# Other ranks in the instruction planner of a four-layer decoder trunk, two lead tiles in the second MLP and an earlier sigmoid table

## The chip, the cores and the metric

The kernel runs on one core of a Trainium2 chip. The metric is device time in microseconds (us) of one execution, the median of several runs; one further execution is profiled. TensorE (PE in the profile) does the matmuls and has a separate row for its weight loads (PEld), VectorE is DVE, ScalarE is ACT, GpSimd is POOL, and SyncE (SP) only issues the loads and stores (DMAs). Each engine works through its own queue in order and waits at an instruction until what that instruction needs is there.

## What is computed

The reference is a trunk of four layers over 512 positions, with 16 learned positions put in front (528 in all), at width 1024, in float32. Cut to what matters:

```python
def sq_relu_mlp(h, norm_g, w_up, w_down):
    return jnp.square(jax.nn.relu(rms_norm(h, norm_g) @ w_up)) @ w_down

def conformer_conv_module(...):
    u = rms_norm(h, norm_g) @ pw1_w + pw1_b
    u = u[..., :CONF_DIM] * jax.nn.sigmoid(u[..., CONF_DIM:])
    u = causal_depthwise_conv(u, dw_w, dw_b)
    u = jax.nn.silu(layer_norm(u, ln_g, ln_b))
    return u @ pw2_w + pw2_b

def reference(...):
    h = jnp.concatenate([meta, x], axis=1)
    for layer in range(DEPTH):                 # DEPTH = 2
        if layer % 2 == 0:
            h = h + even_mixer(...)            # one input projection, sliding-window attention
        else:                                  # beside an SSD scan, one output projection
            h = h + conformer_conv_module(...)
        h = h + sq_relu_mlp(...)               # 1024 -> 4096 -> 1024
    return h[:, N_META:]
```

The weights of the two MLPs are most of the work: 4096 x 1024 up and down for each.

## The kernel before, in words

**Tiles and streams.** The positions lie in the free dimension and the features on the partitions. They are split in two streams, A (s = 0, blocks 0 to 2, 272 positions) and B (s = 1, blocks 3 and 4, 256 positions); the second MLP works on 256 of each. The trace names tiles by stage, layer, quarter and stream: up02A is the up projection of layer 0, quarter 2, stream A, dn02A the down projection behind it, pw the two projections of the conformer module, out those of the output projection.

**Precision.** A linear layer is computed in split form: a weight tile of 128 x 1024 (or 128 x 512) is loaded by SP (`wr`, L289), ACT casts it to its high part (`wh`, L280, in `th_cast`), and DVE (L254) or POOL (L256) subtracts to get the low part (`wl`, in `th_low`). An output tile of 128 features is 24 matmuls at L308 for eight k of 128: per k the high part times the high and the low part of the input (nh and nl, or ah and al), then the low weight part times the high input. A stage of eight tiles is 192 matmuls.

**The planner.** No engine's order is written by hand. `Sched` holds threads (Python generators) which offer their next operation. `step` takes the operation that can start first by the planner's costs, among equals the one with the smaller rank (the second argument of `spawn`), then the one that waited longest; what it takes is appended to that engine's queue. An operation with a `late` of LATE (600 ns) is put off by that margin, so that PE does not stand waiting for its input. The matrix stages are the thread `main` (rank 5), the weight loads have rank 0, the casts 1, and the low parts 0 or 4, according to how many split pieces stand ready; each finished tile spawns an evacuation with a rank of its own.

**Banks.** Outputs stand in PSUM. `pmm` gives a stage one of three mm banks or, in the later stages, one of the three bg banks besides: four at most. A bank comes free with the last instruction of the evacuation that reads it. In `mlp` the evacuation of an up tile is DVE (relu, L268, or L261 with the row norm), ACT (square), ACT (cast to ah) and DVE (al, L254). In `prep`, for stages that add to the residual stream, it goes on to nh, nl, h and the sum of squares, DVE's acc being last.

**dense.** `dense` (L462 to L512) runs a stage. With `lead` tiles it starts so many tiles on their first `cut` k's, each in its own bank, and then finishes them one after the other, so that PE has work before the last k's of the input are written. The other tiles follow one at a time. In the second MLP the lead was 4 and the cut 6.

**Norms.** A stage that writes the residual stream also gathers sums of squares. `row_norm` (L530) sums them over the partitions by a matmul into a bank (names st and a key), takes the reciprocal root by ACT's Sqrt and a Newton step on DVE (`rsqrt`), and spreads the result over the partitions by a second matmul whose copy is `rb`. Keys: in0 and in1 for the first layer's input, nx for the first MLP, cn for the conformer module, ln for its layer norm, fn for the second MLP. Sigmoid and Sqrt stand in different tables of ACT, and a change of table shows as ACT_TABLE_LOAD.

**Stages.** `main` runs: the input projection; out for stream A; quarters 0 and 1 of the first MLP for A, beside which the attention (att_a, att_b, att_c) and the SSD scan (ssd_...) of blocks 3 and 4 still run; then, when these are done, the memory pool that they used is closed, a pool for whole weight tiles is opened in its place (`wp`), and out for B begins (L1312 its evacuation); quarters 2 and 3 for A; pw1 for A; the first MLP for B; pw1 for B; pw2 for A; the second MLP for A; pw2 for B; the second MLP for B, which writes the output.

Of the kernel before, what the change touches and what calls it, by code (L numbers as in the profile page):

```python
# [53 lines left out]
LATE = 600.0  # L54
# [11 lines left out]
class Sched:  # L66
# [106 lines left out]
    def spawn(self, gen, prio, name):  # L173

        self.threads.append([gen, prio, None, None, 0, name])
# [55 lines left out]
def trunk(ctx: ExitStack, tc: tile.TileContext, h0, vecs, cmat, atab, atab0, w_in, w_dt, w_out,  # L231
# [86 lines left out]
    def BM(*ms):  # L318
        return MM(ms, LATE)
# [148 lines left out]
    def dense(name, nts, tot, xs, evac, lead=0, cut=0, when=None):  # L468
# [5 lines left out]
        for part in range(2 if lead else 0):  # L474
            for i, n in enumerate(nts[:lead]):
# [17 lines left out]
                if part:  # L493
                    for _, pc in pcs:
                        done_with(*pc[:2])
                    for s in range(len(xs)):
                        spawn(evac(n, s, bs[s]), 1, name + "ev")
        for n in nts[lead:]:
            pcs = []
            for s, x in enumerate(xs):  # L500
                p = yield pmm(name)
                k, i = 0, 0
                while k < tot:
                    if s == 0:
                        pcs.append((yield from piece()))
                    pc = pcs[i]
                    yield from products(p, pc, k, range(k, k + pc[2]), tot, x, 0, when and when[s])
                    if s == len(xs) - 1:
                        done_with(*pc[:2])
                    k += pc[2]  # L510
                    i += 1
                spawn(evac(n, s, p), 1, name + "ev")  # L512

# [3 lines left out]

    def rsqrt(r, t, v):

        yield ACT(t, v, AF.Sqrt)  # L520
        yield VEC(6.2 * cols(r) + 150, lambda: nc.vector.reciprocal(r, t), r, t)
        yield TT(t, r, r, ALU.mult)
        yield TT(t, t, v, ALU.mult)
        yield TS(t, t, -0.5, 1.5, ALU.mult, ALU.add)
        yield TT(r, r, t, ALU.mult)
# [3 lines left out]

    def row_norm(s, a, blocks, eps, key, stay=False):  # L530

# [5 lines left out]
                   for i, c in enumerate(blocks)))  # L537
# [3 lines left out]
        r, t = (small([128, 16], x + key)[:, :nb] for x in ("rs_r", "rs_t"))  # L541
        yield from rsqrt(r, t, v)
        n = sum(blk(c)[1] for c in blocks)
        p = yield bank("bg", "st" + key)
        yield BM(*((p[:, blk(c)[0] - b0:blk(c)[0] - b0 + blk(c)[1]], r[0:blk(c)[1], i:i + 1].to_broadcast([blk(c)[1], 128]),
                    ident[0:blk(c)[1], 0:blk(c)[1]], True, True) for i, c in enumerate(blocks)))
        if stay:
# [674 lines left out]
    def prep(cnt, s, xh_, xl_, g, key, blocks, eps=1e-6):  # L1222
# [19 lines left out]
        def stats():  # L1242
            c0 = blk(blocks[0])[0] - (STREAM[s][0] if key != "fn" else blk(blocks[0])[0])
            yield from row_norm(s, acc[s][:, c0:], blocks, eps, f"{key}{s}")
            done.add(f"{key}{s}")
# [17 lines left out]
    def out_proj(s, pr, early):  # L1263
# [34 lines left out]
        for n in range(8):  # L1298
# [9 lines left out]
            if n == 0:  # L1308
                yield after(f"norm{s}")
                yield from next_inputs(s)  # L1310
                post[0] = pr(s)
            spawn(ev(n, p), 1, f"out{s}ev")  # L1312

# [64 lines left out]
    def main():  # L1378
# [79 lines left out]
        for q in range(NQ):  # L1458
            plan_mlp(1, q, 4 if q == 0 else 0, 6, 2)
        expect([w_p2[n] for n in range(8)], 8)  # L1460
        for q in range(4):
            plan_mlp(1, q, 4 if q == 0 else 0, 6, 2)
        over.append(True)
# [143 lines left out]
        for q in range(4):  # L1607
            yield from mlp(1, q, [(*F[0], *AH[0], add_h if q < 3 else fin)], 4 if q == 0 else 0, 6, 2)
        yield from pause("ln")
        bias[0] = 0.0  # L1610
        yield from pw2(1, *AH[1], prf[1])
        for q in range(4):
            yield from mlp(1, q, [(*F[1], *AH[1], add_h if q < 3 else fin)], 4 if q == 0 else 0, 6, 2)

    with tc.manual_schedule():
        nc.sync.dma_start(vec[:, 0:8], vecs[:, 0:8])
        S.part(vec)[0][0][:, :8] = 2500.0
        for g, p, n in ((main(), 5, "main"), (th_load(), 0, "load"), (th_cast(), 1, "cast"),
                        (th_low(), lambda: 0 if split[0] - used[0] < 3 else 4, "low")):
            spawn(g, p, n)  # L1620
# [86 lines left out]
```

## Time and profile before

| | us |
|---|---|
| median of three runs | 1256.73 (1256.43 to 1256.98) |
| profiled execution | 1257.62 |
| its span on the core | 1255.8 |
| PE busy | 1226.9 |
| DVE busy | 858.7 |
| ACT busy | 679.4 |
| POOL busy | 547.3 |

The span goes from the first to the last instruction; the profiled execution's own time has 1.8 us around it. PE is busy almost throughout, so what is to be read in this profile is where PE stands still, which engine ended the wait, and how long stages of the same size took.

### The profile page before, as it was taken

How to read it: one execution, taken by the hardware profiler on the slowest of the kernel's cores; microseconds unless marked ns; L12 is line 12 of the kernel's file. 1: busy time of each engine (PE TensorE's matmuls, PEld its weight loads, DVE VectorE, ACT ScalarE, POOL GpSimd, SP SyncE). 2: the span in 40 equal slices, each digit the busy share in tenths (PEclk: the TensorE clock that was granted, in tenths of full speed). 3: DMA queues.
4: the chain of work that ended last, by engine and by line, in shares of the span. 5: the costliest groups of instructions: out<-in, count | busy, mean ns of one | idle time of the engine just before them, and what ended most of it. 6: DMA issues, size and time to landing. Idle time of an engine off the chain costs nothing.

```text
span 1255.8 us, 25614 instructions
## 1 busy us (share of the span) xinstructions
PE 1226.9 (98%) x9939; PEld 1182.2 (94%) x9939; DVE 858.7 (68%) x1916; ACT 679.4 (54%) x1272; POOL 547.3 (44%) x338
## 2 busy tenths in 40 slices
PE   9999998999999989999999999999999999899998
PEld 7999886898899989999999999999999999899998
DVE  6845775787765565648989864588998426575664
ACT  7654245675664653654544577555446645544542
POOL 0122331344441221248888878887887880000000
PEclk9999998999999999999999999999999999999999
DMA  6322112343346745546556556555565566456562
GB/s 188 108 83 85 35 51 60 108 125 97 122 142 215 227 154 176 177 136 186 185 183 185 184 169 194 162 185 165 172 196 172 172 217 182 154 182 187 183 194 92
DMA packets 79961, 194.38 MB, mean 155 GB/s; under 512 B 8912, under 2 KB 16608, under 8 KB 79840
## 3 DMA queue, kind: packets, MB, share of 16 engines
q1 hardware_dynamic: 79840, 192.75, 49.4%
q8 instruction: 78, 1.28, 0.4%
q14 instruction: 43, 0.35, 0.1%
HBM read 190.62 MB, written 2.10 MB: 153 GB/s over the span
## 4 chain that ended last, share of the span: by engine, by line
PE 91%; DVE 4%; ACT 3%; issue 1%; DMA 0%; SPq 0%; DVEq 0%; ACTq 0%
PE in L308 11%; PE pw L308 9%; PE out L308 5%; PE up00A L308 2%; PE up01A L308 2%; PE dn02A L308 2%; PE dn01A L308 2%; PE up03A L308 2%; PE dn00A L308 2%; PE up10A L308 2%; PE up03B L308 2%; PE dn03B L308 2%; PE dn13B L308 2%; PE dn11B L308 2%; PE dn10B L308 2%; PE dn11A L308 2%
## 5 line engine op out<-in xcount | busy, mean ns | idle before, releaser
L256 POOL TENSOR_TENSOR wl<-wr,wh 128x1024 fp32r<-128x1024 f32 (+1 forms) x290 | 515.9, 1797 | 430.9 <-ACT wh L280 366.0
L280 ACT CAST wh<-wr 128x512 fp32r<-128x512 f32 (+1 forms) x494 | 383.7, 801 | 310.7 <-PE in L308 31.0
L254 DVE TENSOR_TENSOR wl<-wr,wh 128x512 fp32r<-128x512 f32 (+1 forms) x204 | 189.5, 940 | 90.4 <-ACT wh L280 89.2
L261 DVE SCALAR_TENSOR_TENSOR conv<-U,vec,conv 128x256 f32<-128x256 f32 x464 | 210.9, 484 | 5.0
L308 PE MATMUL in<-xh,wh 128*128 128x272 f32 (+1 forms) x384 | 103.5, 297 | 1.3 <-ACT wh L280 0.7
L308 PE MATMUL in<-xl,wh 128*128 128x272 f32 (+1 forms) x384 | 100.8, 289 | 0.2
L308 PE MATMUL pw<-nh,wh 128*128 128x256 f32 (+1 forms) x320 | 80.1, 285 | 2.5 <-ACT sg L276 2.5
L308 PE MATMUL pw<-nl,wh 128*128 128x256 f32 (+1 forms) x320 | 79.9, 284 | 0.0
L308 PEld LDWEIGHTS in<-xh,wh 128*128 128x128 f32 x384 | 73.4, 191 | 6.3 <-issue 2.8
L308 PEld LDWEIGHTS in<-xl,wh 128*128 128x128 f32 x384 | 73.4, 191 | 1.5 <-DVE xl L261 1.4
L308 PE MATMUL in<-xh,wl 128*128 128x272 f32 (+1 forms) x384 | 67.1, 291 | 0.0
L308 PEld LDWEIGHTS pw<-nh,wh 128*128 128x128 f32 x320 | 60.3, 189 | 2.9 <-ACT sg L276 2.9
L308 PEld LDWEIGHTS pw<-nl,wh 128*128 128x128 f32 x320 | 60.3, 188 | 0.0
L308 PEld LDWEIGHTS in<-xh,wl 128*128 128x128 f32 x384 | 55.1, 192 | 2.1 <-issue 1.2
L308 PE MATMUL pw<-nh,wl 128*128 128x256 f32 (+1 forms) x320 | 49.1, 285 | 0.0
L308 PEld LDWEIGHTS pw<-nh,wl 128*128 128x128 f32 x320 | 42.9, 189 | 0.0
L276 ACT ACT_TABLE_LOAD x27 | 34.6, 1283 | 6.4 <-DMA hin<-in_h 4.1
L308 PE MATMUL out<-xh,wh 128*128 128x272 f32 (+1 forms) x128 | 33.1, 289 | 0.6 <-ACT h L280 0.6
L308 PE MATMUL out<-xl,wh 128*128 128x272 f32 (+1 forms) x128 | 32.6, 285 | 0.0
L254 DVE TENSOR_TENSOR pw<-pw,rb 128x272 f32<-128x272 f32 (+1 forms) x32 | 14.1, 441 | 26.0 <-PE pw L308 26.0
L308 PEld LDWEIGHTS out<-xh,wh 128*128 128x128 f32 x128 | 24.2, 189 | 2.0 <-ACT h L280 0.9
L308 PEld LDWEIGHTS out<-xl,wh 128*128 128x128 f32 x128 | 24.1, 189 | 0.1
(596 smaller groups left out, 3662.4 us busy)
## 6 DMA issues: line engine op xcount, KB each, us to landing
wr<-in_w_up SPq DMA_DIRECT2D x84, 512.0 KB, 3.6
wr<-in_w_dn SPq DMA_DIRECT2D x84, 512.0 KB, 4.0
wr<-in_w_up SPq DMA_DIRECT2D x88, 256.0 KB, 4.3
wr<-in_w_dn SPq DMA_DIRECT2D x88, 256.0 KB, 4.1
wr<-in_w_p SPq DMA_DIRECT2D x36, 512.0 KB, 3.7
wr<-in_w_in SPq DMA_DIRECT2D x48, 256.0 KB, 2.9
wr<-in_w_out SPq DMA_DIRECT2D x36, 256.0 KB, 2.7
wr<-in_w_p SPq DMA_DIRECT2D x24, 256.0 KB, 4.7
```

Source lines behind the costliest of these rows:

```text
L254: ways = [("V", 1.04 * n + 145, lambda: nc.vector.tensor_tensor(o, a, b, op=op), sb(a) and sb(b))]
L256: ways.append(("G", 2.17 * n + 170, lambda: nc.gpsimd.tensor_tensor(o, a, b, op=op), True))
L261: lambda: nc.vector.scalar_tensor_tensor(o, a, s, b, op0=op0, op1=op1), sb(a) and sb(b))],
L276: return Op([("A", ns, lambda: nc.scalar.activation(o, a, f, **kw), False)], aps(o, accum), aps(a, scale, bias), table=TABLE.get(f, 0))
L280: return Op([("A", 0.836 * cols(o) + 192, lambda: nc.scalar.copy(o, a), False)], [o], [a])
L308: nc.tensor.matmul(o, lhsT=l, rhs=r, start=st, stop=sp)
```

## The change

It touches five things, all of them in the Python that plans the order; the arithmetic of the result stays, and PE gets the same matmuls.

1. Evacuations that `dense` spawns, and those of `out_proj`, get rank 0.5 in place of 1.
2. `rsqrt` and `row_norm` take an activation function `then`. For the key cn, a sigmoid of one column of a constant is put on ACT right behind the Sqrt, its result unused.
3. The second matmul of `row_norm` has the margin LATE only for the keys fn, nx and ln; for in0, in1 and cn it has none.
4. The second MLP's first quarters have two lead tiles in place of four, in the weight plan and in the stage.
5. The low parts have rank 1 in place of 0 when fewer than three split pieces stand ready.

```diff
@@ -494,7 +494,7 @@
                     for _, pc in pcs:
                         done_with(*pc[:2])
                     for s in range(len(xs)):
-                        spawn(evac(n, s, bs[s]), 1, name + "ev")
+                        spawn(evac(n, s, bs[s]), 0.5, name + "ev")
         for n in nts[lead:]:
             pcs = []
             for s, x in enumerate(xs):
@@ -509,15 +509,17 @@
                         done_with(*pc[:2])
                     k += pc[2]
                     i += 1
-                spawn(evac(n, s, p), 1, name + "ev")
+                spawn(evac(n, s, p), 0.5, name + "ev")
     def small(shape, tag, bufs=1):
         return tmp.tile(shape, F32, tag=tag, bufs=bufs, name=nm(tag))
-    def rsqrt(r, t, v):
+    def rsqrt(r, t, v, then=None):
         yield ACT(t, v, AF.Sqrt)
+        if then is not None:
+            yield ACT(small([128, 1], "then"), ident[:, 0:1], then)
         yield VEC(6.2 * cols(r) + 150, lambda: nc.vector.reciprocal(r, t), r, t)
         yield TT(t, r, r, ALU.mult)
         yield TT(t, t, v, ALU.mult)
@@ -527,7 +529,7 @@
     rb = [keep.tile([128, 272], F32, name=f"rb{s}") for s in range(2)]
     acc = [keep.tile([128, 272], F32, name=f"acc{s}") for s in range(2)]
-    def row_norm(s, a, blocks, eps, key, stay=False):
+    def row_norm(s, a, blocks, eps, key, stay=False, then=None):
         nb = len(blocks)
@@ -539,11 +541,12 @@
         yield TS(v, p[:, :nb], 1.0 / D, eps, ALU.mult, ALU.add)
         drop(p)
         r, t = (small([128, 16], x + key)[:, :nb] for x in ("rs_r", "rs_t"))
-        yield from rsqrt(r, t, v)
+        yield from rsqrt(r, t, v, then)
         n = sum(blk(c)[1] for c in blocks)
         p = yield bank("bg", "st" + key)
-        yield BM(*((p[:, blk(c)[0] - b0:blk(c)[0] - b0 + blk(c)[1]], r[0:blk(c)[1], i:i + 1].to_broadcast([blk(c)[1], 128]),
-                    ident[0:blk(c)[1], 0:blk(c)[1]], True, True) for i, c in enumerate(blocks)))
+        yield MM([(p[:, blk(c)[0] - b0:blk(c)[0] - b0 + blk(c)[1]], r[0:blk(c)[1], i:i + 1].to_broadcast([blk(c)[1], 128]),
+                    ident[0:blk(c)[1], 0:blk(c)[1]], True, True) for i, c in enumerate(blocks)],
+                 LATE if key[:2] in ("fn", "nx", "ln") else 0.0)
         if stay:
             return p
         yield CP(rb[s][:, :n], p[:, :n])
@@ -1241,7 +1244,7 @@
         def stats():
             c0 = blk(blocks[0])[0] - (STREAM[s][0] if key != "fn" else blk(blocks[0])[0])
-            yield from row_norm(s, acc[s][:, c0:], blocks, eps, f"{key}{s}")
+            yield from row_norm(s, acc[s][:, c0:], blocks, eps, f"{key}{s}", False, AF.Sigmoid if key == "cn" else None)
             done.add(f"{key}{s}")
         return f
@@ -1309,7 +1312,7 @@
                 yield after(f"norm{s}")
                 yield from next_inputs(s)
                 post[0] = pr(s)
-            spawn(ev(n, p), 1, f"out{s}ev")
+            spawn(ev(n, p), 0.5, f"out{s}ev")
     def mlp(layer, q, streams, lead=0, cut=4, dlead=0, dcut=6):
@@ -1456,10 +1459,10 @@
         expect([w_p1[n] for n in range(16)], 8, 4, 6)
         expect([w_p2[n] for n in range(8)], 8)
         for q in range(NQ):
-            plan_mlp(1, q, 4 if q == 0 else 0, 6, 2)
+            plan_mlp(1, q, 2 if q == 0 else 0, 6, 2)
         expect([w_p2[n] for n in range(8)], 8)
         for q in range(4):
-            plan_mlp(1, q, 4 if q == 0 else 0, 6, 2)
+            plan_mlp(1, q, 2 if q == 0 else 0, 6, 2)
         over.append(True)
         wide[0] = 1
         yield from out_proj(1, pr, False)
@@ -1605,18 +1608,18 @@
             yield DMA(out[n * 128:n * 128 + 128, c0 - NM:c0 - NM + w], o[:, :w], 128)
             drop(o)
         for q in range(4):
-            yield from mlp(1, q, [(*F[0], *AH[0], add_h if q < 3 else fin)], 4 if q == 0 else 0, 6, 2)
+            yield from mlp(1, q, [(*F[0], *AH[0], add_h if q < 3 else fin)], 2 if q == 0 else 0, 6, 2)
         yield from pause("ln")
         bias[0] = 0.0
         yield from pw2(1, *AH[1], prf[1])
         for q in range(4):
-            yield from mlp(1, q, [(*F[1], *AH[1], add_h if q < 3 else fin)], 4 if q == 0 else 0, 6, 2)
+            yield from mlp(1, q, [(*F[1], *AH[1], add_h if q < 3 else fin)], 2 if q == 0 else 0, 6, 2)
     with tc.manual_schedule():
         nc.sync.dma_start(vec[:, 0:8], vecs[:, 0:8])
         S.part(vec)[0][0][:, :8] = 2500.0
         for g, p, n in ((main(), 5, "main"), (th_load(), 0, "load"), (th_cast(), 1, "cast"),
-                        (th_low(), lambda: 0 if split[0] - used[0] < 3 else 4, "low")):
+                        (th_low(), lambda: 1 if split[0] - used[0] < 3 else 4, "low")):
             spawn(g, p, n)
         while S.threads:
             S.step()
```

Three places show how the order moves. The first is DVE in the first up quarter of the second MLP for stream B: up10B is the tile in PSUM, al the low part of the activation whose instruction frees the bank, wl a low part of weights, rs the row norm's small tiles. Before:

```order
L268 TENSOR_SCALAR up10B_13862<-up10B_13862 128x256
L268 TENSOR_SCALAR up10B_13893<-up10B_13893 128x256
L254 TENSOR_TENSOR wl_13995<-wr_13804,wh_13993 128x1024
L268 TENSOR_SCALAR up10B_13926<-up10B_13926 128x256
L254 TENSOR_TENSOR wl_14013<-wr_13843,wh_14003 128x1024
L268 TENSOR_SCALAR up10B_13952<-up10B_13952 128x256
L254 TENSOR_TENSOR al_5690<-up10B_13862,ah_5689 128x256
L254 TENSOR_TENSOR wl_14024<-wr_13876,wh_14015 128x1024
L254 TENSOR_TENSOR al_5690<-up10B_13893,ah_5689 128x256
```

After:

```order
L268 TENSOR_SCALAR up10B_13862<-up10B_13862 128x256
L268 TENSOR_SCALAR up10B_13897<-up10B_13897 128x256
L523 RECIPROCAL rs_rfn_13942<-rs_tfn_13943 128x2
L254 TENSOR_TENSOR rs_tfn_13943<-rs_rfn_13942 128x2
L254 TENSOR_TENSOR rs_tfn_13943<-rs_tfn_13943,rs_vfn_13937 128x2
L268 TENSOR_SCALAR rs_tfn_13943<-rs_tfn_13943 128x2
L254 TENSOR_TENSOR rs_rfn_13942<-rs_rfn_13942,rs_tfn_13943 128x2
L254 TENSOR_TENSOR al_5690<-up10B_13862,ah_5689 128x256
L254 TENSOR_TENSOR al_5690<-up10B_13897,ah_5689 128x256
L268 TENSOR_SCALAR up10B_13950<-up10B_13950 128x256
L254 TENSOR_TENSOR wl_13991<-wr_13816,wh_13951 128x1024
```

The al of the first lead tile stood behind four relus and two low parts; it now stands behind two relus and the row norm, ahead of the next low part.

The second is DVE in up02A, the third up quarter of the first MLP for stream A. Before:

```order
L261 SCALAR_TENSOR_TENSOR up02A_5695<-up02A_5695,rb_81 128x272
L261 SCALAR_TENSOR_TENSOR up02A_5720<-up02A_5720,rb_81 128x272
L254 TENSOR_TENSOR wl_5771<-wr_5639,wh_5746 128x1024
L268 TENSOR_SCALAR rs_vnx_5791<-stnx_5693 128x2
L254 TENSOR_TENSOR wl_5787<-wr_5652,wh_5774 128x1024
L521 RECIPROCAL rs_rnx_5803<-rs_tnx_5804 128x2
L261 SCALAR_TENSOR_TENSOR up02A_5745<-up02A_5745,rb_81 128x272
L254 TENSOR_TENSOR rs_tnx_5804<-rs_rnx_5803 128x2
L261 SCALAR_TENSOR_TENSOR up02A_5773<-up02A_5773,rb_81 128x272
L254 TENSOR_TENSOR wl_5821<-wr_5658,wh_5818 128x1024
L254 TENSOR_TENSOR rs_tnx_5804<-rs_tnx_5804,rs_vnx_5791 128x2
L254 TENSOR_TENSOR al_5688<-up02A_5695,ah_5687 128x272
```

After:

```order
L261 SCALAR_TENSOR_TENSOR up02A_5695<-up02A_5695,rb_81 128x272
L261 SCALAR_TENSOR_TENSOR up02A_5720<-up02A_5720,rb_81 128x272
L254 TENSOR_TENSOR wl_5771<-wr_5639,wh_5746 128x1024
L268 TENSOR_SCALAR rs_vnx_5790<-stnx_5693 128x2
L261 SCALAR_TENSOR_TENSOR up02A_5745<-up02A_5745,rb_81 128x272
L254 TENSOR_TENSOR al_5688<-up02A_5695,ah_5687 128x272
L254 TENSOR_TENSOR al_5688<-up02A_5720,ah_5687 128x272
L254 TENSOR_TENSOR wl_5809<-wr_5652,wh_5774 128x1024
```

Of the three low parts (wl) that stood ahead of the first al, one is left there.

The third is ACT at the end of dn01A, up to the first cast of out's weights for stream B (128x1024, from the pool that takes the closed one's memory). pt and pmt are the attention's probabilities, copied for block 4's last products att_c, and oh is their result. Before:

```order
L280 CAST wh_5012<-wr_4955 128x512
L280 CAST wh_5032<-wr_4969 128x512
L280 CAST wh_5050<-wr_4983 128x512
L280 CAST wh_5068<-wr_5007 128x512
L280 CAST wh_5085<-wr_5023 128x512
L280 CAST wh_5102<-wr_5041 128x512
L280 CAST wh_5165<-wr_5162 128x1024
```

After:

```order
L280 COPY pmt_5030<-att_b_5026 128x128
L280 CAST wh_5035<-wr_4975 128x512
L280 COPY pt_5051<-att_b_5044 128x512
L280 COPY pt_5066<-att_b_5045 128x512
L280 CAST wh_5056<-wr_5005 128x512
L280 CAST wh_5081<-wr_5032 128x512
L280 COPY pt_5099<-att_b_5090 128x512
L280 COPY pt_5105<-att_b_5091 128x512
L280 CAST oh<-att_c_5043 128x4x128
L280 CAST wh_5165<-wr_5162 128x1024
```

Block 4's attention, which before was done in up01A, now stands right ahead of that cast. On PE its last att_c now comes 24 dense matmuls ahead of the first matmul of out for B; before, it was 308 ahead. The load of those weights on SP waits for PE's att_c, and after the change for ACT's copies too.

## The prediction

> **What bounds the kernel now.** I read the page first, then the chain of waits, then a table of windows over every stretch in which TensorE stands still, and last the timeline of the engines that it waits for. The page:
>
> ```profile
> span 1255.8 us, 25614 instructions
> PE 1226.9 (98%) x9939; PEld 1182.2 (94%) x9939; DVE 858.7 (68%) x1916; ACT 679.4 (54%) x1272; POOL 547.3 (44%) x338
> PE 91%; DVE 4%; ACT 3%; issue 1%; DMA 0%; SPq 0%; DVEq 0%; ACTq 0%
> ```
>
> TensorE (PE) is busy for 98% of the span and makes 91% of the chain that ended last. Its work does not change (the same matmuls in another order), so the change can only win or lose idle time and clock. What a stage costs with neither lost stands in the chain:
>
> ```profile
> 379.76 24.11 PE dn01A L308 x192
> 1116.39 22.69 PE up11B L308 x192
> ```
>
> So a matmul takes 24.11/192 = 0.126 us in stream 0 of the first layer (272 columns) and 22.69/192 = 0.118 us elsewhere (256). Most stages run at that pace. The stretches that do not are few, and the timeline of PE names them; the bracket is the idle time before the matmul and what ended it:
>
> ```profile
> 330.47 0.50 PE L308 MATMUL ssd_d<-R,mgtr 128*128 128x512 f32 x1 [2.27 <-DVE R L254]
> 454.13 0.60 PE L308 MATMUL up02A<-nh,wh 128*128 128x272 f32 x1 [3.16 <-DVE al L254]
> 555.98 0.39 PE L308 MATMUL pw<-nh,wh 128*128 128x272 f32 x1 [1.18 <-ACT sg L276]
> 791.84 0.39 PE L308 MATMUL pw<-nh,wh 128*128 128x256 f32 x1 [1.31 <-ACT sg L276]
> 862.82 0.39 PE L308 MATMUL up10A<-nh,wh 128*128 128x256 f32 x1 [1.78 <-DVE al L254]
> 1060.46 0.39 PE L308 MATMUL pw<-ah,wh 128*128 128x256 f32 x1 [0.93 <-DVE acc L254]
> 1069.42 0.39 PE L308 MATMUL up10B<-nh,wh 128*128 128x256 f32 x1 [1.60 <-DVE acc L254]
> 1080.56 0.39 PE L308 MATMUL up10B<-nh,wh 128*128 128x256 f32 x1 [2.85 <-DVE al L254]
> ```
>
> All but the first wait for a PSUM bank: al, acc and sg are the last instructions that read a finished tile, and the bank is free after them. In the windows (columns: stretch and length, busy time and count of PE, its weight loads, DVE, ACT and POOL, granted clock, DMA share, GB/s) one sees what the waits drag behind them:
>
> ```profile
> 450.97:454.13 3.16, 0.00 (x0) 0.00 (x1) 3.12 (x5) 2.56 (x8) 2.19 (x2) 0.99 0.71 222
> 454.07:457.48 3.41, 3.35 (x15) 3.35 (x16) 1.28 (x6) 0.00 (x0) 0.87 (x1) 0.50 0.87 296
> 863.67:867.08 3.41, 3.41 (x19) 3.41 (x18) 1.95 (x6) 1.84 (x5) 3.41 (x2) 0.50 0.68 184
> 1067.82:1069.42 1.60, 0.00 (x1) 0.00 (x0) 1.19 (x3) 1.58 (x3) 0.00 (x0) 1.00 0.86 225
> 1077.70:1080.56 2.86, 0.01 (x2) 0.00 (x1) 2.86 (x6) 2.86 (x7) 0.00 (x0) 1.00 0.29 64
> 1082.12:1085.53 3.41, 3.41 (x19) 3.41 (x18) 2.07 (x5) 0.41 (x2) 0.00 (x0) 0.50 0.93 306
> 1085.53:1088.94 3.41, 3.41 (x31) 3.41 (x31) 1.25 (x3) 1.57 (x3) 0.00 (x0) 1.00 0.27 105
> 331.19:334.60 3.41, 3.34 (x15) 3.37 (x16) 2.69 (x7) 1.02 (x2) 0.50 (x2) 0.50 0.42 142
> ```
>
> After each idle stretch of 1.78 us or more stands one of 3.41 us with the clock at 0.50: 19 matmuls start in it, against 31 in the next one at 1.00. By count it loses 12 x 0.118 = 1.4 us, by pace 3.41 - 19 x 0.118 = 1.2; I take 1.3 us for each. After the idle 1.60, 1.31 and 1.18 us none follows.
>
> **A rule against this price.** The Trainium skill, "TensorE: Matmul & The Clock Gate", section "HAM oscillation — how this bites in real kernels", warns only of idle gaps of more than about 3.4 us. The trace disagrees: gaps of 1.78 to 3.16 us have their stretch at 0.50. By the page the gain below would be without the four stretches and the loss without its one, 3.9 us less in sum.
>
> **First quarter of the second MLP, lead 4 to 2.** Four lead tiles take all four banks that the stage may hold. The fourth has to wait for the last tile of the stage before (acc, the 1.60), and the fifth for the first lead tile's al. DVE in that wait:
>
> ```profile
> 1077.15 1.23 DVE L254 TENSOR_TENSOR wl<-wr,wh 128x1024 fp32r<-128x1024 f32 x1 [0.41 <-ACT wh L280]
> 1078.62 1.22 DVE L254 TENSOR_TENSOR wl<-wr,wh 128x1024 fp32r<-128x1024 f32 x1
> 1080.09 0.42 DVE L254 TENSOR_TENSOR al<-up10B,ah 128x256 fp32r<-128x256 f32 x1
> ```
>
> The al stands behind two low parts of 1.2 us. After the change the two lead tiles are done 48 matmuls in, the third tile takes a bank that is free, and the fourth, 24 matmuls later, has the one of acc; so the leads' evacuation has two tiles of 2.84 us (24 x 0.118) to run in, and its al stands ahead of the low part. What four leads were for is the cover of the last inputs (nl of the eighth k):
>
> ```profile
> 1063.41 0.28 PE L308 MATMUL up10B<-nh,wh 128*128 128x256 f32 x1
> 1066.91 0.48 DVE L261 SCALAR_TENSOR_TENSOR nl<-pw,vec,nh 128x256 fp32r<-128x256 f32 x1
> 1068.95 0.41 DVE L254 TENSOR_TENSOR acc<-acc,pw 128x256 f32<-128x256 f32 x1
> ```
>
> It is written at 1067.39, 3.98 us after the first matmul. Two leads of six k are 36 matmuls, 4.25 us: enough by 0.27. Gain in up10B: 1.60 + 2.85 + 1.3 = 5.75. In up10A 1.78 + 1.3 = 3.08. Against it, the matmul that sums the row statistics now stands about 40 matmuls (4.7 us) into up10B, while acc ends 1069.36 - 1063.41 = 5.95 us in; the evacuations' rank brings acc forward, and between 0 and 1.2 I take 0.25 of loss.
>
> **Evacuations ahead of low parts (rank 1 to 0.5, low parts 0 to 1).** In up02A the stretch of 3.16 us has DVE busy for 3.12, with three low parts ahead of the al that frees the bank; after, one stands there. Gain 3.16 + 1.3 = 4.46. The 0.93 before the last pw2 tile is an acc of the same kind and goes too, ends 0 and 0.93.
>
> **Early sigmoid table.** The wait for sg holds a table load:
>
> ```profile
> 553.09 1.05 ACT L280 CAST wh<-wr 128x1024 fp32r<-128x1024 f32 x1 [0.99 <-PE pw L308]
> 554.15 1.28 ACT L276 ACT_TABLE_LOAD   x1
> 555.44 0.49 ACT L276 ACTIVATE sg<-pw,vec 128x272 f32<-128x272 f32 x1
> ```
>
> Loaded behind the Sqrt, it lies beside the statistics' DVE steps and the broadcast. Its 1.28 us cover the 1.18 and all but 0.03 of the 1.31: gain 1.18 + 1.28 = 2.46; there is one load as before, only earlier, so nothing is added but a one-column activation.
>
> **The order of the attention and SSD work.** In the first layer these ranks move the chains of blocks 3 and 4 later, by some 70 to 290 of the dense matmuls that they lie beside. In dn00A the wait of 2.27 + 1.3 = 3.57 us for R can go or be replaced, and I count half, 1.8, between 0 and 3.57. At the end it costs: the first loads of out1's weights go into memory that the attention of block 4 held, and SP issues them after its last matmul (att_c). Before, that one stood here, and the loads came long after it:
>
> ```profile
> 363.10 2.10 PE att_c L308 x12
> 403.70 0.28 PE L308 MATMUL out<-oh,wh 128*128 128x256 f32 x1
> wr<-in_w_out SPq DMA_DIRECT2D x3, 512.0 KB, 4.2
> wr<-in_w_up SPq DMA_DIRECT2D x84, 512.0 KB, 3.6
> ```
>
> Now it stands 24 matmuls, 24 x 0.126 = 3.0 us, ahead of out1's first. The load lands 3.6 (whole kernel) to 4.2 us (there) after issue and the cast takes 1.05, so PE idles for 3.6 + 1.05 - 3.0 = 1.65 to 2.25, and on SP all later loads of out1 queue behind. I take 2.0 and, as it is over 1.78, a stretch at half clock: 3.3 us lost, between 1.65 (no stretch) and 3.55. The broadcast matmul of the row norms in0, in1, cn0 and cn1 loses the planner's margin of 600 ns. If its r comes late, the dense matmuls queued behind it on PE wait, up to 0.6 us at four places, 2.4 in all; earlier, it brings rb and so the banks forward. I count nothing, since it stands between dense matmuls and its r comes of a short DVE chain, and leave it to the range.
>
> **The sum.** Gains 5.75 + 3.08 + 4.46 + 0.93 + 2.46 + 1.8 = 18.5; losses 0.25 + 3.3 = 3.55; net 15.0. The profiled execution took 1257.62 us (1.8 around its span) and the median of the runs is 1256.73, 0.9 less: 1257.62 - 15.0 - 0.9 = 1241.7. The forecast's own range: 1241.7 - 1.8 (dn00A whole) - 1.9 (out1 without stretch) = 1238.0, and 2 us for new waits or gains in the input stages and at the broadcasts, which I cannot read: 1236. Upward 1.8 (dn00A nothing), 0.9 (pw2), 1.0 (statistics), 0.25 and 2: 1247.6.
>
> **Rivals.** *The wait turns into one for low parts.* In 450.97:454.13 and 1077.70:1080.56 DVE was busy throughout (3.12 of 3.16, 2.86 of 2.86). A low part put behind evacuations is late for its own matmuls, and PE waits there. Half of what up02A, up10A and up10B give, 13.3/2 = 6.65, stays: 1248.4. Against it, lead 2 spreads the evacuations. Chance 0.15.
>
> *The moved SSD and attention wait more.* The longest wait of that work in the trace is this one:
>
> ```profile
> 213.17 0.47 PE L315 MATMUL att_b<-cm,pm 128*128 128x128 f32 x1 [4.65 <-DVE pm L254]
> ```
>
> If dn00A, with more DVE work in it, gets one like it, 4.65 + 1.3 instead of a gain of 1.8, the time is 7.75 up, 1249.5. Chance 0.10. With the rival before it the two make 1256.1, no change: 0.05.
>
> *The clock is not the gaps' doing.* If stretches at 0.50 come whatever the gaps (the page's rule leaves gaps below 3.4 us free of them), 3.9 us of the sum go: 1245.6. The rows speak against it: each stands right behind a long gap. Chance 0.07.
>
> *Slower: weight preparation falls behind.* Casts keep rank 1 and now stand behind evacuations; each up tile brings two of them, and POOL makes low parts only after the cast:
>
> ```profile
> 1077.02 0.37 ACT L276 ACTIVATE up10B<-up10B 128x256 f32<-128x256 f32 x1
> 1078.55 0.36 ACT L280 CAST ah<-up10B 128x256 fp32r<-128x256 f32 x1
> 554.21 2.36 POOL L256 TENSOR_TENSOR wl<-wr,wh 128x1024 fp32r<-128x1024 f32 x1 [5.64 <-ACT wh L280]
> POOL wl L256 <- ACT wh L280: 366.0, 156, 24.2
> ```
>
> A tile is 2.84 us of matmuls and 2.36 of POOL: 0.48 to spare. If two such steps of ACT, 0.73 us, delay every cast and the buffers do not make it good, 0.25 us is lost per tile; over the 64 tiles of the first MLP's stream 1 and the 24 of pw1 and pw2 beside it that is 22 us, 1263.7. It decides from 0.48 us of delay per tile on. Against it: POOL waits 366.0 us for casts altogether, so there is slack. Chance 0.06.
>
> **How the numbers follow.** Forecast 0.57, low parts 0.15, SSD 0.10, clock 0.07, both of the first 0.05, slower 0.06. Faster by over 0.2% (2.5 us, about what a measurement of this kernel can tell from no change) is 0.57 + 0.15 + 0.10 + 0.07 = 0.89; within it 0.05; slower 0.06. The range goes from 1236 to 1250 and takes in the first three rivals; outside lie 0.11 and the tails of these, 0.2 at most.
>
> **What would show it.** Right: no bank wait (al, acc) of more than 0.5 us in up02A, up10A, pw2 and up10B, no windows at 0.50 there, no table load between the first pw tile and its sg, a new wait of about 2 us on a cast of out1's weights near 400 us, stages up10A and up10B near 24 us. Wrong: PE waits for wl in those stages, a wait of over 3 us in dn00A or dn01A, POOL's wl ending just ahead of the matmuls in the first MLP's stream 1, or stretches at 0.50 without a gap before them.

## The result and the profile after

The changed kernel takes 1238.11 us, the median of four runs (1236.53 to 1238.37), against 1256.86 for the kernel before; the ratio is 0.984, its 95% interval 0.981 to 0.987. The forecast was 1241.7. The profiled execution took 1237.84 us, 19.8 less than that of before.

The page after:

```profile
span 1236.1 us, 25626 instructions
PE 1219.7 (99%) x9939; PEld 1176.1 (95%) x9939; DVE 861.5 (70%) x1915; ACT 683.4 (55%) x1277; POOL 549.5 (44%) x339
PE 92%; DVE 3%; ACT 3%; issue 1%; DMA 1%; SPq 0%; DVEq 0%; ACTq 0%
```

TensorE has the same 9939 matmuls; its busy time fell by 7.2 us (the matmuls at half clock are longer, and there are fewer of them) and the idle time by 12.5. Which stages gave it is read from one window for each, with the columns of the prediction. First before, for up02A, pw1 of stream A, up10A and up10B:

```profile
437.70:468.36 30.66, 27.16 (x204) 26.72 (x203) 19.40 (x34) 16.08 (x34) 4.66 (x4) 0.94 0.49 157
541.00:592.20 51.20, 50.02 (x399) 49.63 (x398) 31.83 (x76) 24.75 (x38) 38.83 (x20) 1.00 0.54 165
848.70:875.80 27.10, 25.32 (x203) 25.12 (x202) 22.84 (x62) 15.83 (x31) 19.52 (x11) 0.94 0.50 154
1063.41:1093.68 30.27, 25.82 (x204) 25.41 (x203) 18.02 (x36) 16.79 (x33) 0.00 (x0) 0.94 0.42 139
```

Then the same four after:

```profile
434.90:460.50 25.60, 25.31 (x203) 25.09 (x202) 18.84 (x35) 17.26 (x34) 2.91 (x3) 1.00 0.59 189
533.30:583.80 50.50, 50.30 (x400) 49.93 (x399) 32.74 (x76) 25.25 (x39) 38.72 (x20) 1.00 0.53 167
838.80:863.00 24.20, 23.84 (x203) 23.67 (x202) 22.39 (x57) 16.31 (x31) 19.63 (x11) 1.00 0.55 174
1049.20:1073.84 24.64, 24.25 (x204) 23.88 (x204) 18.27 (x36) 16.53 (x33) 0.00 (x0) 1.00 0.55 177
```

The lengths fall by 5.1, 0.7, 2.9 and 5.6 us, and the mean clock of three of them goes from 0.94 to 1.00. VectorE's busy time in each is the same within 1 us: it does the same work in another order. Of PE's waits after, these are the two longest, and what is left at up02A and up10B:

```profile
213.42 0.47 PE L315 MATMUL att_b<-cm,pm 128*128 128x128 f32 x1 [4.36 <-DVE pm L254]
400.58 0.38 PE L308 MATMUL out<-oh,wh 128*128 128x256 f32 x1 [1.91 <-ACT wh L280]
441.40 0.40 PE L308 MATMUL up02A<-nh,wh 128*128 128x272 f32 x1 [0.29 <-DVE acc L254]
1054.90 0.35 PE L308 MATMUL stfn<-cm,acc 128*128 128x1 f32 x2 [0.39 <-DVE acc L254]
```

None of the eight waits that the prediction listed is left. The start of the input stage is worse off in this execution: four waits of 0.25 to 1.23 us (0.71 at most before), and half clock from 10.07 to 16.90 us, which the trace of before lacks:

```profile
7.29 0.39 PE L308 MATMUL in<-xh,wh 128*128 128x272 f32 x1 [1.23 <-ACT wh L280]
10.07:13.49 3.42, 2.93 (x12) 2.39 (x11) 3.34 (x8) 3.17 (x9) 0.00 (x0) 0.50 1.09 362
```

The 1.91 at the start of out is new and is the one forecast (2.0). SP issues the loads of those weights 0.08 us after the last att_c has ended on PE (395.66):

```profile
395.74 6.41 SPq L289 DMA_DIRECT2D wr<-in_w_out  x6
```

The loads of those weights in the DMA view of that stretch (KB each, us to landing):

```profile
wr<-in_w_out SPq DMA_DIRECT2D x3, 512.0 KB, 3.7
```

and the cast behind them on ACT, which started when the first load had landed:

```profile
399.49 1.57 ACT L280 CAST wh<-wr 128x1024 fp32r<-128x1024 f32 x2 [3.20 <-DMA wr<-in_w_out]
```

The table load now stands behind the Sqrt, at 539.98 us, 6.9 us ahead of the first sg:

```profile
539.98 1.28 ACT L276 ACT_TABLE_LOAD   x1
541.27 0.20 ACT L276 ACTIVATE then<-cm 128x1 f32<-128x1 f32 x1
546.85 0.48 ACT L276 ACTIVATE sg<-pw,vec 128x272 f32<-128x272 f32 x1
```

### The profile page after: what moved, and what is told of

Its sections match the earlier page's. It is cut to its first block, busy times and chain, and to the rows that moved or that the text cites. A ratio compares the mean times of both kernels' runs of the same rounds, so it can differ in the third digit from the quotient of the medians.

```text
span 1236.1 us, 25626 instructions
## 1 busy us (share of the span) xinstructions
PE 1219.7 (99%) x9939; PEld 1176.1 (95%) x9939; DVE 861.5 (70%) x1915; ACT 683.4 (55%) x1277; POOL 549.5 (44%) x339
## 4 chain that ended last, share of the span: by engine, by line
PE 92%; DVE 3%; ACT 3%; issue 1%; DMA 1%; SPq 0%; DVEq 0%; ACTq 0%
PE in L308 11%; PE pw L308 9%; PE out L308 5%; PE dn00A L308 2%; PE up00A L308 2%; PE up01A L308 2%; PE up03A L308 2%; PE dn02A L308 2%; PE dn12A L308 2%; PE up03B L308 2%; PE dn13B L308 2%; PE dn12B L308 2%; PE dn11B L308 2%; PE dn10B L308 2%; PE dn11A L308 2%; PE dn03B L308 2%
```

## The experiments

The theory to test was the sum of the prediction: each wait for a bank goes by the part of the change that was meant for it, the late attention costs a bare load, and each long gap drags 1.3 us of half clock behind it. The rivals were that ranks alone, or leads alone, do it, and that the clock follows something else. Three of the kernels below (the leads alone, the ranks alone, and the change without its leads) order one step of the arithmetic otherwise: the first tiles of dn10A, two or four of them, are scaled by acc before the squared row norm is written there, so these tiles, and the result behind them, hold other numbers. The instructions and their sizes are the same, and TensorE has no wait in dn10A in any of the three or in the changed kernel. Seven others (one lead tile, the margin alone, both with idle times, low parts at rank 1 alone, and the two with rank 1 from out on) have two lines that the code below doesn't show: every such scaling waits until the squared row norm is written. Before and in the changed kernel it comes in that order without them. What these lines alone do to the time was not measured.

**The leads alone.** Four lines, each as this one:

```diff
-            plan_mlp(1, q, 4 if q == 0 else 0, 6, 2)
+            plan_mlp(1, q, 2 if q == 0 else 0, 6, 2)
```

> The kernel before with the lead of the second MLP's first quarters 2 instead of 4 and nothing else. Theory (four leads use up the four banks; with two the evacuation has time whatever its rank): the waits on acc (1.60) and al (1.78, 2.85) and the two stretches at half clock go, 3.08 + 5.75 = 8.8 us, so 1248 us; up02A keeps its wait of 3.2. Rival (the order on VectorE decides, and one low part still stands ahead of the first al in up10B): up10B keeps a wait of 1.2 us or more with its stretch at half clock, a gain of 6 us at most, 1251 or more.

Measured: 1249.53 us, ratio 0.994 (0.993 to 0.996), 7.7 us less. PE's waits in up10A and in up10B:

```profile
861.97 0.39 PE L308 MATMUL up10A<-nh,wh 128*128 128x256 f32 x1 [0.53 <-DVE al L254]
1067.12 0.58 PE L308 MATMUL stfn<-cm,acc 128*128 128x1 f32 x4 [0.75 <-DVE acc L254]
```

Both bank waits of up10B are gone although a low part still stands ahead of the first al, so the free banks do it and not the order on VectorE. The theory holds, with 1.1 us less than forecast: 0.53 of a bank wait is left, and 0.75 for the statistics, which the prediction had bounded by 1.2.

**The ranks alone.**

```diff
-                spawn(evac(n, s, p), 1, name + "ev")
+                spawn(evac(n, s, p), 0.5, name + "ev")
...
-            spawn(ev(n, p), 1, f"out{s}ev")
+            spawn(ev(n, p), 0.5, f"out{s}ev")
...
-                        (th_low(), lambda: 0 if split[0] - used[0] < 3 else 4, "low")):
+                        (th_low(), lambda: 1 if split[0] - used[0] < 3 else 4, "low")):
```

> The kernel before with the ranks alone: evacuations 0.5, low parts 1, lead still 4. Theory: up02A gains 4.5, the last pw2 tile 0.9, the first layer up to the second out stage 3.1 as in the changed kernel; with one low part ahead of the first al instead of two, up10B's 2.85 shrinks by about 1.2 to 1.6 but the wait for the fourth bank (acc) stays near 1.6 less 0.5: some 10 to 11 us in all, 1246. Rival (ranks alone free the banks in time, leads do nothing): up10A and up10B run clean as well, 17 us, 1240.

Measured: 1243.21 us, 0.989 (0.988 to 0.990), 14.0 us less, between the two expectations. The ranks clear up02A and the first layer, and most of the second MLP's waits too:

```profile
1067.78 0.39 PE L308 MATMUL up10B<-nh,wh 128*128 128x256 f32 x1 [1.60 <-DVE al L254]
```

The wait for the fourth bank, which I expected to stay, went: at rank 0.5 the last pw2 tile's acc comes early enough. In up10A 0.86 of 1.78 is left. Neither wait has half clock behind it; the wait at the start of out, 1.69 us here, has.

**The change without its leads.** The four lines of the first experiment, put back in the changed kernel.

> The changed kernel with the lead back at 4 and all else as changed. Theory: the fourth lead tile waits for acc again (about 1.1 to 1.6 us) and the fifth for al (up to 1.6 behind one low part) in up10B, up10A waits 1 to 1.8, with a stretch at half clock where a window of the clock holds enough idle time: 4 to 7 us back, 1242 to 1245. Rival (the ranks alone suffice): 1238, up10A and up10B within 25 us each.

Measured: 1240.51 us, ratio to before 0.987 (0.985 to 0.989), 2.4 us above the changed kernel and so less than forecast. The waits are 0.87 and 1.61 for al, 2.5 together:

```profile
853.14 0.39 PE L308 MATMUL up10A<-nh,wh 128*128 128x256 f32 x1 [0.87 <-DVE al L254]
1064.88 0.39 PE L308 MATMUL up10B<-nh,wh 128*128 128x256 f32 x1 [1.61 <-DVE al L254]
```

So leads and ranks overlap: alone they give 7.7 and 14.0, and together with the rest 18.8. Beside the ranks the leads are worth about 2.4 us, not the 8.8 that the prediction put down to them. By the times alone these 2.4 are not sure (the intervals 0.985 to 0.989 and 0.981 to 0.987 overlap); the waits of 2.5 us in the trace are what speaks for them.

**One lead tile in the changed kernel.** `2 if q == 0` becomes `1 if q == 0` in those four lines.

> The changed kernel with one lead tile instead of two. Theory (leads must cover the 4.0 us until nl of the eighth k is written; 18 matmuls cover 2.1): TensorE waits about 1.9 us for nh or nl in up10A and in up10B, with a stretch at half clock where a window of the clock holds enough of it: 1241.9 to 1244.5 us. Rival (only the banks count): 1238.

Measured: 1239.01 us, ratio to before 0.986 (0.984 to 0.988), which can't be told from the changed kernel. The trace can: no wait in up10A, and two in up10B.

```profile
1050.43 0.39 PE L308 MATMUL up10B<-nh,wh 128*128 128x256 f32 x1 [0.63 <-ACT nh L276]
1051.71 0.38 PE L308 MATMUL up10B<-nl,wh 128*128 128x256 f32 x1 [0.89 <-DVE nl L261]
```

The theory's time is missed. Its mechanism (PE waits for nh and nl) holds for up10B, with 1.5 us of waits and no half clock behind them, where the last nl is written 4.4 us after the first matmul. In up10A it comes 2.2 us after, and 18 matmuls cover that; I had taken the 4.0 us of one stage for both.

**The early sigmoid alone.** The edits of `rsqrt`, `row_norm` and `stats`.

> The kernel before with the early sigmoid alone. Theory: the two waits for sg (1.18 and 1.31) go and nothing else changes: 2.2 to 2.5 us, 1254.3. Rival (the table load delays other work of ScalarE, casts or the copy of rb, by the same 1.28): 1 us or less, 1256.

Measured: 1256.93 us, 0.999 (0.997 to 1.000): no difference that can be told. The theory holds for the waits and misses the time. Both waits for sg are gone, and the two pw stages are shorter by 1.3 and 1.4 us. But in this execution the first out stage began 0.85 us later (223.77 against 222.92; the input stage had half clock from 8.21 to 15.04 us), and up10B got a stretch at half clock more than before (after the 1.61 for acc) and lost 1.3:

```profile
1066.33:1069.75 3.42, 2.01 (x17) 2.01 (x18) 1.37 (x5) 2.06 (x4) 0.00 (x0) 1.00 0.83 299
1069.76:1073.17 3.41, 3.41 (x19) 3.41 (x18) 0.62 (x4) 0.00 (x0) 0.00 (x0) 0.50 0.02 7
```

**The margin of the second row-norm matmul alone.**

```diff
-        yield BM(*((p[:, blk(c)[0] - b0:blk(c)[0] - b0 + blk(c)[1]], ...
+        yield MM([(p[:, blk(c)[0] - b0:blk(c)[0] - b0 + blk(c)[1]], ...
+                 LATE if key[:2] in ("fn", "nx", "ln") else 0.0)
```

> The kernel before with the margin of the second row-norm matmul taken away for in0, in1 and cn alone. Theory: no wait of TensorE changes by more than 0.5 us, 1256.7 us within 0.2%. Rival (it brings rb, and with it the banks of pw1, forward or makes TensorE wait for r): 1 to 2.4 us either way, in the first stages or in pw1.

Measured: 1256.09 us, 0.998 (0.997 to 0.999), 1.1 us less by the medians. No wait of TensorE went: 3.16, 1.18, 1.31, 1.78, 1.61 and 2.87 are all there, and one of the first layer is 0.2 longer. The theory's part on the waits holds; the small gain is not explained by them. What its profile shows is in up10B, and it bears on the clock. The wait there is as long as before (2.87 to 2.85):

```profile
1083.58 0.39 PE L308 MATMUL up10B<-nh,wh 128*128 128x256 f32 x1 [2.87 <-DVE al L254]
```

Yet no stretch at half clock follows it in the windows, and the stage is 28.8 us instead of 30.3:

```profile
1078.71:1082.12 3.41, 2.00 (x17) 1.79 (x16) 2.72 (x5) 3.07 (x7) 0.00 (x0) 1.00 0.00 0
1082.12:1085.53 3.41, 1.95 (x16) 1.95 (x17) 3.41 (x7) 3.21 (x8) 0.00 (x0) 1.00 0.78 238
1085.53:1088.94 3.41, 3.41 (x31) 3.41 (x31) 2.17 (x6) 1.07 (x3) 0.00 (x0) 1.00 0.92 305
```

All changes of the clock in a run lie on one grid of 3.41 us, in each of the fourteen traces within 0.01 us. Here an edge of that grid (1082.12) cuts the wait in 1.41 and 1.46 us of idle time, and neither window is followed by half clock. Before, the edge stands at the same time (1082.11), but the stage begins 3.0 us earlier, so that the grid lies otherwise on the wait:

```profile
1075.28:1078.70 3.42, 2.42 (x21) 2.21 (x19) 2.42 (x5) 3.00 (x6) 0.00 (x0) 1.00 0.00 0
1078.70:1082.11 3.41, 1.55 (x13) 1.55 (x14) 3.41 (x7) 3.41 (x9) 0.00 (x0) 1.00 0.66 204
```

It cut the same wait in 1.0 and 1.86, and the window 1082.12 to 1085.53 that the prediction shows ran at 0.50.

**Idle times put in.** Between the stages of the second MLP, in the changed kernel, `main` makes TensorE wait for a chain on another engine; first on VectorE, then on ScalarE (shown):

```diff
+        yield MM([(p[:, 0:64], ident, ident[:, 0:64], True, True)])
+        yield CP(z, p[:, 0:64])
+        for _ in range(n):
+            yield CP(z, z)
+        yield MM([(p[:, 64:128], ident, z, True, True)])
```

> The changed kernel with 14 idle times put between the stages of the second MLP: TensorE waits for a chain of small instructions on VectorE, about 1.2 to 3 us each. Theory (the clock looks at fixed windows of 3.41 us, and the window after one with more than about half of it idle runs at 0.50): a gap costs its length, and 1.3 us more only where 1.8 us or more of it lie in one window; gaps of 1.8 to 2.8 us that are split by a window's edge cost their length alone. Rival (the length alone decides, with a limit between 1.6 and 1.8): every gap above 1.8 us has a stretch at 0.50 behind it.

Measured: 1423.52 us. This run can't decide: every idle time was 4.2 us or more, and at the first, ahead of dn10A, TensorE also stood 53 us for the convolution behind the layer norm's input (Y), which VectorE made in one go. All had half clock behind them, which both theories say.

> The changed kernel with 14 shorter idle times between the stages of the second MLP: TensorE waits for copies of 64 columns on ScalarE, about 0.8 to 3.5 us each. Theory (fixed windows of 3.41 us on the clock; the window after one with more than about half idle runs at 0.50): stretches at 0.50 stand only behind windows with 1.4 to 1.8 us or more idle; a gap of 1.8 to 2.8 us split by an edge into two lesser parts has none. Rival (the length of a gap alone decides): each gap above 1.8 us has one.

Measured: 1368.92 us, with thirteen idle times of 1.2 to 5.7 us besides that first one. Three of them on PE:

```profile
1232.82 0.32 PE L308 MATMUL gap<-gz,cm 128*128 128x64 f32 x1 [3.15 <-ACT gz L280]
1206.32 0.32 PE L308 MATMUL gap<-gz,cm 128*128 128x64 f32 x1 [1.45 <-ACT gz L280]
993.95 0.32 PE L308 MATMUL gap<-gz,cm 128*128 128x64 f32 x1 [2.05 <-ACT gz L280]
```

The windows of the grid around the first:

```profile
1227.57:1230.99 3.42, 2.10 (x19) 1.96 (x17) 2.67 (x4) 2.77 (x7) 0.00 (x0) 1.00 0.53 161
1230.99:1234.40 3.41, 1.58 (x13) 1.58 (x14) 1.78 (x4) 1.50 (x7) 0.00 (x0) 1.00 0.73 226
1234.41:1237.82 3.41, 3.41 (x18) 3.41 (x17) 0.00 (x0) 0.00 (x0) 0.00 (x0) 0.50 0.44 169
```

The 3.15 is cut in 1.32 and 1.83; the window after the first part runs at 1.00 and the one after the second at 0.50. The 2.05, with 1.90 in one window, has its stretch, the 1.45 has none. By itself this run does not decide either: all idle times of 2.05 us or more have a stretch and those of 1.73 or less none, which the rival also says; no gap above 1.8 us fell so that both its parts were small. Over all runs, from 15 us after the start on and apart from the two cases in the last section, windows at full clock with 1.33 us idle or less were never followed by half clock and those with 1.83 or more always; from 1.41 to 1.80 both occurred (their edges are known from the clock's changes alone). The rival, a limit on the length alone, falls by the 2.87 of the run above. Idle time in a window is not the whole rule either: behind 1.41 us there was half clock (early sigmoid alone), behind the 1.46 above there was none.

**Low parts back at rank 0 in the changed kernel.**

```diff
-                        (th_low(), lambda: 1 if split[0] - used[0] < 3 else 4, "low")):
+                        (th_low(), lambda: 0 if split[0] - used[0] < 3 else 4, "low")):
```

> The changed kernel with the low parts back at rank 0. On TensorE the last att_c now stands 54 dense matmuls ahead of the second out stage instead of 24, 54 x 0.126 = 6.8 us. Theory (the wait at the start of that stage is the load that may only be issued behind att_c, 3.6 to 4.2 us, and its cast, 1.05): 6.8 covers both, the wait of 1.9 goes and the time is 1236 us; up02A, up10A, up10B as in the changed kernel. Rival (low parts at rank 0 push the evacuations back as before): the waits on al return in up02A or up10B, 2 us or more, 1240.

Measured: 1239.74 us, ratio to before 0.987 (0.985 to 0.988). The wait at the start of out is gone, as the theory said: its first matmul follows dn01A's last directly. But a wait of 3.30 appears at the second tile of up02A, with half clock behind it. The time is the rival's; the wait is for acc, the last evacuation of out, and not for al:

```profile
438.98 0.57 PE L308 MATMUL up02A<-nh,wh 128*128 128x272 f32 x1 [3.30 <-DVE acc L254]
```

**Low parts at rank 1 alone**, in the kernel before (the same line the other way).

> The kernel before with the low parts at rank 1 and nothing else. The last att_c stands directly ahead of the second out stage. Theory: load 3.6 to 4.2, cast 1.05 and the way between the engines lie bare, 4.7 to 5.5 us idle and a stretch at half clock, 1.3; the waits in up02A (3.2), up10A and up10B stay as before; the first layer up to there gains 3 to 4 as in the changed kernel: in all 1258 to 1260 us. Rival (that wait is of the store of weights, not of att_c): about 2 us idle as in the changed kernel, 1255.

Measured: 1259.63 us, 1.003 (1.002 to 1.004): slower, as expected. Block 4's attention ends directly ahead of out, and the whole load and cast lie bare:

```profile
403.80 0.43 PE L308 MATMUL out<-oh,wh 128*128 128x256 f32 x1 [4.72 <-ACT wh L280]
```

With att_c 0, 24 and 54 matmuls ahead the wait is 4.72, 1.91 and 0, and in all three traces SP issues the first load 0.07 or 0.08 us after att_c's end; so it is the load behind att_c.

**Rank 1 only from out on, and an earlier residual load.** In the changed kernel:

```diff
-                        (th_low(), lambda: 1 if split[0] - used[0] < 3 else 4, "low")):
+                        (th_low(), lambda: (1 if over else 0) if split[0] - used[0] < 3 else 4, "low")):
...
             p, k = (yield pmm(f"out{s}")), first
+            if not early:
+                spawn(fetch(n), -1, f"out{s}ev")
```

> The changed kernel with two edits: low parts have rank 0 until the second out stage begins and 1 from there on, and that stage's residual tiles (ut) are loaded when their matmuls begin instead of when they end. Theory (rank 1 for low parts costs 1.9 us at the start of that stage and gains nothing before it; and the last tiles' evacuation waited for its ut, not for VectorE): no wait at the start of out, none over 0.5 us at the start of up02A, 1235 to 1236 us. Rival (the wait at the start of up02A is VectorE's, three low parts in a row of 4 us): 2 to 3.3 us idle there with a stretch at half clock, 1239 to 1240, as with the low parts at rank 0 throughout.

Measured: 1240.81 us, ratio to before 0.987 (0.985 to 0.988). My theory fell and the rival was right: the start of out is clean, and in up02A 3.20 us are left. VectorE there:

```profile
435.89 0.42 DVE L254 TENSOR_TENSOR acc<-acc,out 128x256 f32<-128x256 f32 x1 [0.71 <-ACT out L276]
436.85 4.05 DVE L254 TENSOR_TENSOR wl<-wr,wh 128x1024 fp32r<-128x1024 f32 x3 [0.53 <-ACT wh L280]
```

Three low parts, 4.05 us, stand ahead of the last tile's evacuation. They stand there in the changed kernel too, but TensorE comes later by the 1.91 that it waited before, and only 0.29 is left of them. Taking the wait at the start of out away moves it to the stage's end.

**The same with low parts on GpSimd from out on.**

```diff
         over.append(True)
         wide[0] = 1
+        bias[0] = 3000.0
```

> The kernel of the run before with late rank 1 and early ut, and besides the planner's penalty for low parts on VectorE at 3000 ns from the second out stage on (600 before, 3000 from pw1 on), so that GpSimd makes them there and no low part stands among the evacuations on VectorE. Theory (the wait at the start of up02A is three low parts in a row on VectorE ahead of the last evacuation): both the wait at the start of out (1.9) and the one in up02A (3.2) are gone, 1235 to 1236 us. Rival (GpSimd, 2.4 us for a 128x1024 piece and 3.0 us of matmuls for one, falls behind in out, whose tiles are one and a half pieces): TensorE waits for low parts there, 1239 or more.

Measured: 1237.88 us, ratio to before 0.985 (0.983 to 0.987), the same as the changed kernel and neither of the expectations: TensorE does not wait for low parts. Both waits are gone, and pw1 begins at 529.6 us instead of 533.3. There a new one takes 3.2 of the 3.7 us back, that of the statistics of cn on PE, with a stretch at half clock:

```profile
536.17 0.47 PE L308 MATMUL stcn<-cm,acc 128*128 128x1 f32 x3 [1.92 <-DVE acc L254]
```

The sums of squares that it waits for, in the view of the tile sqh (shortest, median and longest in ns, first and last start):

```profile
L254 DVE TENSOR_TENSOR acc<-acc,sqh x28: 420/435/2648, 7.3 to 534.7; 128x272 f32<-128x272 f32 x21, 128x256 f32<-128x256 f32 x7
```

and POOL at that time:

```profile
531.91 5.24 POOL L256 TENSOR_TENSOR wl<-wr,wh 128x1024 fp32r<-128x1024 f32 x3 [2.45 <-ACT wh L280]
```

This add, of two operands outside PSUM, takes 0.435 us as a rule and here up to 2.65, beside POOL's low parts. In the changed kernel too, the one add that lies wholly beside such a low part is long, 1.10 us. That POOL is the cause was not tested by a run of its own. No version that I ran is measurably better than the changed kernel.

## Why the prediction came out right, and where it was off

**The waits for banks.** Right in place and size. Forecast 5.5 (5.75 less 0.25), 3.08 and 4.46 us for up10B, up10A and up02A; measured 5.6, 2.9 and 5.1. The wait of 0.93 went as well. What was wrong is to whom the gain belongs: the step "lead 4 to 2" was given 8.8 us, but with the ranks changed it is worth about 2.4, since a bank that comes free earlier and a bank that is not asked for remove the same wait.

**The table.** Both waits went, 2.1 us shorter stages (0.7 and 1.4) against 2.46. By its time the run with the early sigmoid alone could not show it; its stages do (1.3 and 1.4).

**The first layer.** This term of the sum was mis-sized: forecast 1.8 gained less 3.3 lost, measured 3.1 us gained up to the first matmul of out (403.70 before, 400.58 after) and 0.3 lost within it. Two steps did it. All of the gain lies behind 219.59 us, where both kernels start the same att_c: the wait of att_b ahead of it is 0.29 shorter, but TensorE comes to it 0.54 later. In dn00A I counted half of 3.57 and all of it went. At the start of out the wait was as forecast (1.91 to 2.0), but "as it is over 1.78, a stretch at half clock" failed:

```profile
395.77:399.18 3.41, 2.91 (x24) 2.69 (x22) 0.69 (x1) 0.51 (x1) 0.00 (x0) 1.00 0.67 214
399.18:402.60 3.42, 1.97 (x14) 1.77 (x15) 2.04 (x3) 1.57 (x2) 0.00 (x0) 1.00 0.81 310
402.60:406.01 3.41, 3.41 (x31) 3.41 (x31) 2.44 (x4) 2.56 (x4) 0.00 (x0) 1.00 0.93 317
```

An edge at 399.18 cuts the wait in 0.5 and 1.45, and the window behind runs at 1.00. Those 1.3 us, the other 1.8 of dn00A, and two small waits (0.63 in the first out stage, now 0.25, and 0.29 in dn00A, now gone) make up 3.7 of the 4.3 between forecast and measurement there; for the rest no wait shows.

That the stretch stayed away is luck of this execution. In the five other traces where att_c stands as in the changed kernel, the wait is 1.69 to 2.19 us and has half clock behind it each time. The first of the kernels with idle times has the same 1.91:

```profile
399.79 0.39 PE L308 MATMUL out<-oh,wh 128*128 128x256 f32 x1 [1.91 <-ACT wh L280]
398.19:401.61 3.42, 1.76 (x12) 1.56 (x13) 1.84 (x3) 2.03 (x3) 0.00 (x0) 1.00 0.92 332
401.61:405.02 3.41, 3.41 (x18) 3.41 (x17) 2.77 (x4) 1.98 (x4) 0.00 (x0) 0.50 0.93 316
```

**The clock.** The price of 1.3 us for a stretch stands: with the same waits, up10B is 28.8 us without it and 30.3 with it, 1.5. The rule that I read from before, a limit on a gap's length between 1.60 and 1.78, was wrong: what fits the traces is idle time within a fixed window, the two cases of the last section apart. Between 1.41 and 1.80 us of it something more decides, and that stays open. Two figures of the working are off too. The stretch of dn00A stands in the sum by half, so without stretches the sum is 3.25 us less, not 3.9; and out without its stretch is 1.65 us by the prediction's own bounds, not 1.9. The Trainium skill, "TensorE: Matmul & The Clock Gate", section "What's actually happening", says that the hardware watches a free-running window of 4096 cycles, about 3.4 us; the grid of 3.41 us in these runs agrees, and so does its place in the span, which differs from trace to trace (only before and the margin alone have the same). Its table has the clock fall after an idle window; here 1.83 us of idle time in a window of 3.41 were always enough, and once 1.41.

**The rivals.** In the changed kernel TensorE has no wait of more than 0.2 us for a low part, so the first rival did not come. What the runs show at out is the opposite order: low parts that still stand ahead of the last evacuation, 3.2 us where the start of out is clean and 0.29 in the changed kernel. The SSD work did not wait more. Weight preparation did not fall behind in the first MLP's stream B: the stages from up00B to dn03B start and end with the same lengths within 0.1 us.

## What to carry to other kernels

Two remedies for one wait don't add up: price each with the other in place, or run each alone and both. Before counting a removed wait as gain, look for what is late next at that place; here the late load, the low parts on VectorE and the statistics stood in line behind each other, and clearing the first two brought the third. In these traces waits of 1.6 to 2.9 us stand with and without a stretch at half clock behind them, so their price depends on where they fall on the clock's grid; differences of 1 to 2 us between two kernels want several runs and a look at the clock.

## What the runs showed of the hardware

The runs of one kernel scatter with the clock that they got: those of the kernel with the early sigmoid alone go from 1251.19 us at a mean granted clock of 0.994 to 1258.39 at 0.986. That this is the place of the grid in each run is likely, but not shown, as there is one trace of each kernel. There are stretches without any idle time in front as well. In the run with the margin alone (the profiled execution was its slowest, 1259.12 us) the input stage had them from 122.98 to 133.22 us, and TensorE was busy throughout the window ahead:

```profile
119.57:122.98 3.41, 3.41 (x25) 2.36 (x24) 1.27 (x4) 2.25 (x4) 1.76 (x3) 1.00 0.46 137
122.98:126.40 3.42, 3.42 (x16) 3.08 (x17) 0.90 (x7) 0.96 (x3) 0.53 (x2) 0.50 0.05 19
```

The run with rank 1 from out on and the earlier residual load had one at nearly the same place, 123.56 to 126.97 us, also behind a window without idle time. What sets these off stays open. In half clock the clock also seems slower to come back when the next window holds a little idle time (windows at 0.50 with 0.7 or 0.8 us idle were followed by another at 0.50 in all four cases, those with 0.2 or less by full clock in all but the two of the run above), but no run was made for that.
